# Low parts of the gates' and low-rank factors padded to 128 rows in a two-layer trunk kernel

## The chip, the cores and the metric

The kernel runs on one core of one Trainium2 chip. The metric is the device time of one execution in microseconds (us). TensorE is called PE, its weight loads PEld, VectorE DVE, ScalarE ACT, GpSimd POOL, and SyncE, which issues most transfers, SP.

## The reference

Two layers act on a sequence of 1024 frames with 1024 channels, in float32, each inside `x + norm(mixer(norm(x)))`. Layer 0 runs two mixers on parts of one projection: RG-LRU and HGRN2. Layer 1 is RWKV-7. Cut to what the change touches:

```python
# layer 0, RG-LRU: a causal convolution over 4 frames, then gates in 16 blocks of 64 channels
xblk = xc.reshape(bsz, seq, 16, 64)
gate_r = sigmoid(einsum("bsni,nij->bsnj", xblk, w_a) + b_a)
gate_i = sigmoid(einsum("bsni,nij->bsnj", xblk, w_x) + b_x)
log_a = -8 * gate_r * softplus(-lam)
h = linear_scan(exp(log_a), sqrt(-expm1(2 * log_a)) * (gate_i * xc))
...
# layer 1, RWKV-7: decay and learning rate from factors of rank 64
w_log = -softplus(-(w0 + tanh(mixes[4] @ w1) @ w2)) - 0.5
decay = exp(-exp(w_log))
iclr = sigmoid(a0 + (mixes[5] @ a1) @ a2)
```

The gates' matrices are 64x64, and `w2` and `a2` have 64 rows. Both are the short products of this case. The rest of layer 1 is a delta-rule state per head, worked out in chunks of 64 frames.

## The kernel before

Every float32 product is made of several passes on PE. A number is split into a high part that PE takes exactly (`hi`, rounded by a copy on ACT) and the rest (`lo`, a subtraction); a product then is high by high, high by low and low by high. A dense product of 128 output channels by 512 frames (`dense_t2`, L160 to L162) is 8 x 3 such passes, each 128 rows by 128 columns of weights against 512 columns. Weights come from memory in units; `load_unit` (L131 to L135) loads two tiles of 128x1024, makes the high part on ACT and the low part on POOL.

**Short factors.** With only 64 rows, the first two passes go into one: the rows 64 to 127 of the array take the same weights once more, and the moving tile holds the high part in one half and the low part in the other. So high by high and high by low are one pass of 128 rows (L644 for the gates, L1160 and L1163 for the low-rank factors). Low weights by high data is a pass of 64 rows, which uses one half of the array's rows (L645, L1161, L1164); which half depends on the block, `r = 64h to 64h+63`.

**The gates, `rglru` (L586 on).** The 8 tiles of 128 channels (`e`) are worked in four groups (`j`) of two. For each `e` and each half `th` of the frames: the dense product into PSUM, a copy to `XP` on ACT (L629), the convolution on DVE (L632, L635) into `xc`, the split of `xc` into `xs` (L641, L642), the two gate passes for each `h` on PE, and tanh on ACT (L647), then L648. There are four `xc` buffers, so all are taken in one group. After that come the second dense product of the group (the SiLU gate, L655 and L656), and for the four instances a chain on ACT and DVE (L661 to L665) into the tile `T`, one square root for all four (L667), the multiplications by `T` (L670), the scans (L671), a product (L674), and the transfer of the result to memory (`mgd`). `T` and `a2` are the last tiles of the pool `rg`.

**After it, `out0`.** The output projection of layer 0 multiplies the 16 tiles of `mgd`, in the order k = 8 to 15, then 0 to 7. For the first half of the frames each is loaded (L696, at raised priority) into a buffer of the pool `ut` (8 buffers, at the other end of the memory), split on ACT (L149) and DVE (L150), and used in passes L720 to L722. The first pass of each PSUM bank belongs to k = 8.

**The low-rank factors, `prep` (L1151 on).** Layer 1 makes 16 preparations, one for each `e` and `th`, spread over the dense products for k: a preparation begins with its four short passes into two PSUM tiles (L1160, L1161 for the decay, L1163, L1164 for the learning rate). A tanh (L1167) writes `SG`; DVE adds 1 and scans it into `GC` (L1173, L1174); ACT writes two exponentials of `GC`, `E1` (L1179) and `E2` (L1181), the second into SG's own buffer. `E2` is read by `BT` on DVE (L1195) and `KTt` on POOL (L1201). 32 passes of 64x64 (L1208) multiply BT into PSUM; ACT copies them to `AB` (L1212), and SP writes AB out in two transfers (`abf`, L1219). `SG` and `AB` have two buffers each. Passes of a 128x64 tile (L1228) add sums over heads. The first pieces of the following product use the tag `AB` for their output.

**What sets the order.** The program is written in the order of its loops, with generators that interleave parts by hand. A planner then places each instruction in the queue of its engine by a simulated run of the program, and inserts the waits; each queue is served in its order on the chip. Tiles live in pools; a pool's memory is reused by later pools, and a tile whose bytes belonged to an earlier tile waits for that tile's last reader. Pools on the left are stacked upwards, those marked right downwards.

Of the kernel before, what the change touches and what calls it, by code (L numbers as in the profile page):

```python
# [7 lines left out]
F32 = mybir.dt.float32  # L8
F32R = mybir.dt.float32r
# [7 lines left out]
P = 128  # L17
S = 1024
D = 1024
KT = D // P  # L20
# [25 lines left out]
class Net:  # L46
# [539 lines left out]
    def rglru(self, cx, uh, ul):  # L586
        tc, nc, a = self.tc, self.nc, self.a

        c = sp = cx.enter_context(self.pool("rgc", 1))
        lam = self.vec[:, VIDX["lam"]:VIDX["lam"] + KT]  # L590
# [21 lines left out]
        for bn in ("ba", "bx"):  # L612
            t = c.tile([P, KT], F32, name="h" + bn)
            for h in range(2):
                r = slice(64 * h, 64 * h + 64)
# [4 lines left out]
        for j in range(4):  # L620
            wx = self.unit() if j else None
            inst = []
            for e2 in range(2):
                e = 2 * j + e2
                XP = rp.tile([P, 4 + S], F32, name="XP", bufs=2)
                nc.gpsimd.memset(XP[:, 0:4], 0.0)
                for th in range(2):
# [11 lines left out]
                    for h in range(2):  # L639
                        r, r2 = slice(64 * h, 64 * h + 64), slice(64 - 64 * h, 128 - 64 * h)  # L640
                        nc.vector.tensor_copy(xs[r, h], xc[r])  # L641
                        nc.vector.tensor_sub(xs[r2, h], xc[r], xs[r, h].bitcast(F32))  # L642
                        ps = self.pss.tile([P, HALF], F32, name="sm")
                        nc.tensor.matmul(ps, lhsT=self.gh[:, e, h], rhs=xs[:, h], start=True, stop=False)  # L644
                        nc.tensor.matmul(ps, lhsT=self.gl[r, e], rhs=xs[r, h], start=False, stop=True)  # L645
                        for i, q in ((0, r), (1, r2)):
                            nc.scalar.activation(g[i][r], ps[q], AF.Tanh, scale=0.5, bias=hb[i][q, e:e + 1])  # L647
# [3 lines left out]
            for e2 in range(2):  # L651
                for th in range(2):
                    ps = self.dense_t(wg, e2, uh, ul, th)
# [238 lines left out]
    def layer1_proj(self):  # L892
# [12 lines left out]
        with ExitStack() as cx:  # L905
            mp = self.mx
            with ExitStack() as c2:
                lp = c2.enter_context(self.pool("lora", 1))

                self.l2h = [lp.tile([P, D], F32R, name=f"l2h{i}") for i in range(2)]  # L910
                self.l2l = lp.tile([P, D], F32R, name="l2l")
                self.LT = [lp.tile([P, S], F32R, name=f"LT{i}") for i in range(2)]
                with ExitStack() as c3:
# [4 lines left out]
                    for i in range(2):  # L918
                        r, r2 = slice(64 * i, 64 * i + 64), slice(64 - 64 * i, 128 - 64 * i)
                        nc.gpsimd.tensor_copy(self.l2h[i][r], l2[r])  # L920
                        nc.gpsimd.tensor_copy(self.l2h[i][r2], l2[r])
                        nc.gpsimd.tensor_sub(self.l2l[r], l2[r], self.l2h[i][r].bitcast(F32))
                    self.lora_parts(0, self.LT0)
# [19 lines left out]
                with ExitStack() as c3:  # L943
# [18 lines left out]
                    order = [(j, th) for j in range(2) for th in range(2)] + [(2, 0), (3, 0), (2, 1), (3, 1)]  # L962
                    w, self.mt, self.vgb, self.vgt = {}, kp, 2, "AB"
                    self.mixt = "KK"
# [15 lines left out]
                    for i in range(6):  # L980
                        run = advance()
                        self.vgt = ("AB", "R", "KP")[i // 2]
                        next(vg)
                        next(v1, None)
                        if i < 4:
                            next(v1, None)
# [164 lines left out]
    def prep(self, kp, e, th, pk):  # L1151
# [8 lines left out]
        nc.tensor.matmul(pw, lhsT=self.l2h[0][:, es], rhs=LT[0][:, sl], start=True, stop=False)  # L1160
        nc.tensor.matmul(pw, lhsT=self.l2l[0:64, es], rhs=LT[0][0:64, sl], start=False, stop=True)  # L1161
        pa = self.pss.tile([P, HALF], F32, name="l")
        nc.tensor.matmul(pa, lhsT=self.l2h[1][:, es], rhs=LT[1][:, sl], start=True, stop=False)  # L1163
        nc.tensor.matmul(pa, lhsT=self.l2l[64:128, es], rhs=LT[1][64:128, sl], start=False, stop=True)  # L1164

# [43 lines left out]
        if (e, th) == (KT - 1, 1):  # L1209
            self.norms(kp)  # L1210
        AB = kp.tile([P, 8, 64], F32, name="AB")
        nc.scalar.copy(AB, ps)  # L1212
# [410 lines left out]
```

## Time and profile before

| | us |
|---|---|
| median of 3 runs | 1886.89 |
| lowest and highest of them | 1884.31, 1889.57 |
| the profiled execution: its own time | 1885.01 |
| the profiled execution: first to last instruction (span) | 1882.9 |

| busy in the profiled execution | us | share of the span |
|---|---|---|
| PE | 1737.0 | 92% |
| PE weight loads | 1462.9 | 78% |
| DVE | 1212.2 | 64% |
| ACT | 795.6 | 42% |
| POOL | 695.8 | 37% |

The mean granted clock of TensorE is 0.95 of full speed.

How to read the lines: a row of the timeline has the start in us, the duration in us, the engine, the line of the kernel, the operation, output and inputs by the program's names, the part of the array in rows*columns (PE only), the shapes, and how many instructions are merged; in brackets the idle time of the engine ahead of it and what ended it. The ends of PE's products are modelled and overlap the following ones, so two starts tell more than a duration. "SPq" is the issue of a transfer. A row of the table of stretches has, for each engine, the busy time and the count of instructions in it. A row for one line gives the count, the shortest, median and longest duration in ns, and the first and last start.

### The profile page before, as it was taken

How to read it: one execution, taken by the hardware profiler on the slowest of the kernel's cores; microseconds unless marked ns; L12 is line 12 of the kernel's file. 1: busy time of each engine (PE TensorE's matmuls, PEld its weight loads, DVE VectorE, ACT ScalarE, POOL GpSimd, SP SyncE). 2: the span in 40 equal slices, each digit the busy share in tenths (PEclk: the TensorE clock that was granted, in tenths of full speed). 3: DMA queues.
4: the chain of work that ended last, by engine and by line, in shares of the span. 5: the costliest groups of instructions: out<-in, count | busy, mean ns of one | idle time of the engine just before them, and what ended most of it. 6: DMA issues, size and time to landing. Idle time of an engine off the chain costs nothing. (4 is left out here: it accounts for less than half of the span.)

```text
span 1882.9 us, 36336 instructions
## 1 busy us (share of the span) xinstructions
PE 1737.0 (92%) x14418; PEld 1462.9 (78%) x14418; DVE 1212.2 (64%) x2213; ACT 795.6 (42%) x1550; POOL 695.8 (37%) x618
## 2 busy tenths in 40 slices
PE   8989989999899999999999999978679999997888
PEld 6879789787897777777878766668678998875776
DVE  6485483675847889745354686786593434359985
ACT  5322222323226655445454765764453433432221
POOL 5534232333222212465434244554441425425430
PEclk9999999999899999999999999979878998988989
DMA  5101101111022111365235276654565655544531
GB/s 181 45 23 46 56 19 63 46 35 41 18 73 85 53 60 67 125 238 169 101 123 185 89 171 167 173 130 113 121 164 139 170 148 165 156 132 150 181 106 62
DMA packets 218313, 206.56 MB, mean 110 GB/s; under 512 B 133280, under 2 KB 162208, under 8 KB 218144
## 3 DMA queue, kind: packets, MB, share of 16 engines
q1 hardware_dynamic: 216992, 200.04, 35.5%
q0 software_dynamic: 1152, 4.19, 0.7%
q8 instruction: 114, 1.87, 0.4%
q14 instruction: 55, 0.45, 0.1%
HBM read 136.22 MB, written 67.96 MB: 108 GB/s over the span
## 5 line engine op out<-in xcount | busy, mean ns | idle before, releaser
L135 POOL TENSOR_TENSOR wl<-w,wh 128x1024 fp32r<-128x1024 f32 x110 | 276.5, 2520 | 291.6 <-ACT wh L133 283.2
L160 PE MATMUL mm<-xh,wh 128*128 128x512 f32 x768 | 306.3, 400 | 0.2
L162 PE MATMUL mm<-xh,wl 128*128 128x512 f32 x768 | 305.3, 398 | 0.0
L161 PE MATMUL mm<-xl,wh 128*128 128x512 f32 x768 | 304.1, 396 | 0.0
L184 PE MATMUL mm<-wh,xh 128*128 128x256 f32 x560 | 169.8, 304 | 7.5 <-ACT xh L149 3.7
L160 PEld LDWEIGHTS mm<-xh,wh 128*128 128x128 f32 x768 | 146.0, 190 | 35.3 <-issue 3.6
L162 PEld LDWEIGHTS mm<-xh,wl 128*128 128x128 f32 x768 | 145.9, 190 | 34.5 <-issue 4.1
L161 PEld LDWEIGHTS mm<-xl,wh 128*128 128x128 f32 x768 | 145.9, 190 | 33.2 <-issue 3.4
L186 PE MATMUL mm<-wh,xl 128*128 128x256 f32 x560 | 166.4, 300 | 4.9 <-DVE xl L150 4.9
L133 ACT CAST wh<-w 128x1024 fp32r<-128x1024 f32 x112 | 117.7, 1051 | 124.2 <-PE mm L161 54.8
L185 PE MATMUL mm<-wl,xh 128*128 128x256 f32 x560 | 165.7, 296 | 0.0
L184 PEld LDWEIGHTS mm<-wh,xh 128*128 128x128 f32 x560 | 114.5, 205 | 10.7 <-ACT xh L149 4.3
L186 PEld LDWEIGHTS mm<-wh,xl 128*128 128x128 f32 x560 | 113.6, 204 | 7.0 <-DVE xl L150 6.3
L185 PEld LDWEIGHTS mm<-wl,xh 128*128 128x128 f32 x560 | 114.2, 204 | 0.9
L803 DVE SCALAR_TENSOR_TENSOR mix<-ut,vec,mix 128x512 f32<-128x512 f32 x64 | 62.5, 985 | 39.9 <-ACT mix L802 39.1
L1438 POOL TENSOR_TENSOR BS<-BK,egc 128x1024 f32<-128x1024 f32 x16 | 31.7, 1980 | 139.5 <-PE pt L1443 70.7
L184 PE MATMUL po<-wh,xh 128*128 128x256 f32 x256 | 75.7, 296 | 1.6 <-DVE vg L1021 1.6
L420 DVE COPY_PREDICATED ST<-m_l,sm 64x128 f32<-64x128 uint8 x224 | 72.5, 337 | 5.5
L185 PE MATMUL po<-wl,xh 128*128 128x256 f32 x256 | 75.2, 294 | 0.0
L186 PE MATMUL po<-wh,xl 128*128 128x256 f32 x256 | 74.8, 292 | 0.0
L1428 PE MATMUL pg<-GM,BK 64*128 64x128 f32 x512 | 58.0, 308 | 9.4 <-DMA BK<-bkd 4.8
L1295 DVE TENSOR_TENSOR PR<-YP,BL 128x64 f32<-128x64 f32 (+14 forms) x60 | 57.5, 973 | 11.2 <-POOL BL L1285 10.4
(378 smaller groups left out, 4332.6 us busy)
## 6 DMA issues: line engine op xcount, KB each, us to landing
w<-in_W SPq DMA_DIRECT2D x112, 512.0 KB, 3.8
ard<-AR SPq DMA_DIRECT2D x16, 512.0 KB, 4.1
BK<-bkd SPq DMA_DIRECT2D x16, 512.0 KB, 3.7
vd<-vg SPq DMA_DIRECT2D x32, 256.0 KB, 2.7
GM<-ard SPq DMA_DIRECT2D x32, 256.0 KB, 4.4
x<-in_x SPq DMA_DIRECT2D x8, 512.0 KB, 9.8
mgd<-sgq SPq DMA_DIRECT2D x16, 256.0 KB, 2.1
ut<-mgd SPq DMA_DIRECT2D x16, 256.0 KB, 4.1
```

The lines of the kernel that those rows point to most:

```text
L133: nc.scalar.copy(hi, w)
L135: (nc.vector if first else nc.gpsimd).tensor_sub(lo, w, hi.bitcast(F32))
L160: nc.tensor.matmul(ps, lhsT=wh[:, c:c + P], rhs=a, start=(k == 0), stop=False)
L161: nc.tensor.matmul(ps, lhsT=wh[:, c:c + P], rhs=b, start=False, stop=False)
L162: nc.tensor.matmul(ps, lhsT=wl[:, c:c + P], rhs=a, start=False, stop=(k == KT - 1))
L184: nc.tensor.matmul(ps, lhsT=a, rhs=h, start=(k == 0), stop=False)
L185: nc.tensor.matmul(ps, lhsT=a, rhs=l, start=False, stop=False)
L186: nc.tensor.matmul(ps, lhsT=b, rhs=h, start=False, stop=(k == KT - 1))
L420: nc.vector.copy_predicated(d, m, x)
L803: nc.vector.scalar_tensor_tensor(out, sh, self.v(f"mu{p}", k), out, ALU.mult, ALU.add)
L1295: nc.vector.tensor_mul(fv(PR, 0, [[16 * n, 2], [n, 16], [1, n]]), fv(YP, 0, [[256, 2], [16, 16], [1, n]]), fv(BL, i, [[256, 2], [0, 16], [ ...
L1428: nc.tensor.matmul(ps[h][:, q, :], lhsT=BK[hs, eg * 4 + q, :], rhs=GM[hs, h, eg * 4 + q, :], start=True, stop=True)
```

## The change

The gates' low factor `gl` stays as it was, and `rglru` makes from it, at its start and on POOL, a tile `gl2` of 128 rows for each `e` and `h`: one half of the rows holds the low part, the other half is zero. The pass L645 then takes all 128 rows of `xs`, high and low part. The rows that held nothing are multiplied by zero.

The low-rank factors get two tiles `l2l` in place of one, each with the half that isn't used set to zero on POOL, and the passes L1161 and L1164 take all 128 rows. The second `l2l` needs 4 KB per partition. `AB` no longer has a tile: the copy L1212 writes into SG's buffer, and the pieces that used the tag `AB` use `SG`.

```diff
     def rglru(self, cx, uh, ul):
+        gl = cx.enter_context(self.pool("rgl", 1)).tile([P, KT, 2, P], F32R, name="gl2")
+        for h in range(2):
+            r, r2 = slice(64 * h, 64 * h + 64), slice(64 - 64 * h, 128 - 64 * h)
+            nc.gpsimd.memset(gl[r2, :, h].bitcast(F32), 0.0)
+            nc.gpsimd.tensor_copy(gl[r, :, h], self.gl[r].bitcast(F32))
...
-                        nc.tensor.matmul(ps, lhsT=self.gl[r, e], rhs=xs[r, h], start=False, stop=True)
+                        nc.tensor.matmul(ps, lhsT=gl[:, e, h], rhs=xs[:, h], start=False, stop=True)
...
-                self.l2l = lp.tile([P, D], F32R, name="l2l")
+                self.l2l = [lp.tile([P, D], F32R, name=f"l2l{i}") for i in range(2)]
...
-                        nc.gpsimd.tensor_sub(self.l2l[r], l2[r], self.l2h[i][r].bitcast(F32))
+                        nc.gpsimd.memset(self.l2l[i][r2].bitcast(F32), 0.0)
+                        nc.gpsimd.tensor_sub(self.l2l[i][r], l2[r], self.l2h[i][r].bitcast(F32))
...
-                    w, self.mt, self.vgb, self.vgt = {}, kp, 2, "AB"
+                    w, self.mt, self.vgb, self.vgt = {}, kp, 2, "SG"
...
-                        self.vgt = ("AB", "R", "KP")[i // 2]
+                        self.vgt = ("SG", "R", "KP")[i // 2]
...
-        nc.tensor.matmul(pw, lhsT=self.l2l[0:64, es], rhs=LT[0][0:64, sl], start=False, stop=True)
+        nc.tensor.matmul(pw, lhsT=self.l2l[0][:, es], rhs=LT[0][:, sl], start=False, stop=True)
...
-        nc.tensor.matmul(pa, lhsT=self.l2l[64:128, es], rhs=LT[1][64:128, sl], start=False, stop=True)
+        nc.tensor.matmul(pa, lhsT=self.l2l[1][:, es], rhs=LT[1][:, sl], start=False, stop=True)
...
-        AB = kp.tile([P, 8, 64], F32, name="AB")
+        AB = c3(SG)
         nc.scalar.copy(AB, ps)
```

## The prediction

> **What bounds the kernel now.** First the page's shares, then the table of stretches (PE, PEld, DVE, ACT, POOL busy with counts, then granted clock, DMA share, GB/s), cut where the two groups of changed products run: 577 to 753 us (the gates, L645) and 1064 to 1222 us (the low-rank factors, L1161 and L1164).
>
> ```profile
> PE 1737.0 (92%) x14418; PEld 1462.9 (78%) x14418; DVE 1212.2 (64%) x2213; ACT 795.6 (42%) x1550; POOL 695.8 (37%) x618
> ```
> ```profile
> 545.00:577.00 32.00, 32.00 (x166) 27.23 (x165) 17.72 (x28) 9.08 (x13) 12.74 (x11) 1.00 0.39 132
> 577.00:600.00 23.00, 23.00 (x88) 15.70 (x87) 16.51 (x27) 21.70 (x32) 0.41 (x2) 1.00 0.07 24
> 577.00:753.00 176.00, 168.94 (x671) 125.41 (x669) 147.34 (x193) 114.49 (x154) 32.34 (x17) 0.98 0.17 57
> 764.00:1064.00 300.00, 291.95 (x1309) 238.91 (x1308) 147.89 (x159) 143.17 (x237) 133.45 (x100) 1.00 0.44 150
> 1064.00:1222.00 158.00, 151.35 (x919) 106.31 (x917) 122.31 (x137) 102.06 (x166) 71.61 (x73) 0.98 0.64 160
> 1222.00:1260.00 38.00, 25.93 (x189) 20.72 (x187) 34.59 (x35) 23.47 (x42) 25.49 (x20) 0.64 0.61 159
> ```
>
> PE is busy 96% of both stretches, so it looks like the bound; but DVE is busy 84% and 77% there, and the question is how soon it becomes the bound when PE gets shorter. From 764 to 1064 us PE has 8 us of gaps: what delays PE there delays the end.
>
> Then the products themselves, and the order of time around one.
>
> ```profile
> L645 PE MATMUL sm<-xs,gl x32: 491/493/532, 577.3 to 752.9; 64*128 64x512 f32 x32
> L1161 PE MATMUL l<-LT,l2l x16: 491/498/502, 1065.4 to 1219.8; 64*128 64x512 f32 x16
> L1164 PE MATMUL l<-LT,l2l x16: 491/498/501, 1066.3 to 1222.3; 64*128 64x512 f32 x16
> ```
> ```profile
> 576.79 0.39 PE L161 MATMUL mm<-xl,wh 128*128 128x512 f32 x1
> 576.79 0.19 PEld L644 LDWEIGHTS sm<-xs,gh 128*128 128x128 f32 x1
> 577.02 0.40 PE L644 MATMUL sm<-xs,gh 128*128 128x512 f32 x1
> 577.34 0.18 PEld L645 LDWEIGHTS sm<-xs,gl 64*128 64x128 f32 x1 [0.36 <-issue]
> 577.34 0.49 PE L645 MATMUL sm<-xs,gl 64*128 64x512 f32 x1
> 577.76 0.19 PEld L162 LDWEIGHTS mm<-xh,wl 128*128 128x128 f32 x1 [0.24 <-issue]
> 577.77 0.50 PE L162 MATMUL mm<-xh,wl 128*128 128x512 f32 x1
> 578.11 0.39 PE L644 MATMUL sm<-xs,gh 128*128 128x512 f32 x1
> ```
>
> Durations overlap, so starts are read. Between two full products 0.23 us pass (576.79 to 577.02), and the weights are in before the second starts. With the 64-row product they are 0.32 (577.02 to 577.34), 0.43 (to 577.77) and 0.34 (to 578.11): its weights, and those of the next, are loaded only as it starts. One low product costs 0.09 + 0.20 + 0.11 = 0.40 us above an ordinary one.
>
> **The change part by part.** *Padding.* 64 products lose 0.40 us: 25.6 us of PE time, 12.8 in each stretch. The padded product still streams 512 columns, so it costs the ordinary 0.23. Beside 64x64 products (L1208) a change of tile stays; I take 12.4 for the second stretch.
>
> The Trainium skill, "TensorEngine Tiling (Array Packing)", section "Key Properties", says that every change of tiling mode drains the array, which would hold for the 128x64 tile of L1228 too. Where such a product follows a low one, the exit would stay priced: at most 32 x 0.2 = 6 us less. This case's rows, 0.23 us on both sides, do not show that drain:
>
> ```profile
> 1096.63 0.39 PE L160 MATMUL mm<-xh,wh 128*128 128x512 f32 x1
> 1096.86 0.40 PE L1228 MATMUL n<-sl,sel 128*64 128x512 f32 x1
> 1097.09 0.39 PE L161 MATMUL mm<-xl,wh 128*128 128x512 f32 x1
> ```
>
> *What of the first 12.8 us is on the path.* A group j of the gates has eight pairs of products, each needing xs from DVE (L642). For group 2 and the last pair of group 3:
>
> ```profile
> 672.30 0.47 PE L644 MATMUL sm<-xs,gh 128*128 128x512 f32 x1 [2.59 <-DVE xs L642]
> 693.80 1.40 DVE L642 TENSOR_TENSOR xs<-xc,xs 64x512 fp32r<-64x512 f32 x2
> 697.99 0.39 PE L644 MATMUL sm<-xs,gh 128*128 128x512 f32 x1
> 726.92 0.47 PE L644 MATMUL sm<-xs,gh 128*128 128x512 f32 x1 [2.51 <-DVE xs L642]
> 748.47 1.40 DVE L642 TENSOR_TENSOR xs<-xc,xs 64x512 fp32r<-64x512 f32 x2
> 752.57 0.39 PE L644 MATMUL sm<-xs,gh 128*128 128x512 f32 x1
> ```
>
> At a group's first pair PE waits for DVE (2.59, 2.51 us); at its last, PE is late: xs is ready at 695.20 and 749.87, the product runs 2.79 and 2.70 us later. DVE meanwhile goes on with the next step of its own chain, and the next group's xc buffers come free only after this group's scan. So per group only the lateness at the last pair can be had, some 2.6 us in groups 2 and 3; the rest turns into longer waits at the next first pair. In group 0 ACT is full (21.70 of 23 us), so I estimate 0.3; in group 1, half-way, 0.5. Sum 6 us, between 2 (ACT takes that too) and 12.8.
>
> *Building the padded gate factor.* Two fills and two copies on POOL of 64x1024:
>
> ```profile
> L582 POOL CAST gh<-gates x4: 604/607/622, 35.9 to 53.5; 64x512 fp32r<-64x512 f32 x4
> ```
>
> A copy is twice 0.607, so all four at most 4.9 us. POOL has 19 idle us from 545 to 577, before the first L645; behind them in POOL's queue stand L135's low weight halves and XP's fill. Taken as nothing; without that cover up to 4.9 us. The two fills of l2l stand on POOL with the other preparations of the low-rank factor, ahead of the stage, and are half as much at most: nothing.
>
> *The 8 KB that it occupies.* A `gl2` is 8 x 2 x 128 x 4 = 8,192 bytes per partition, and lies below the gates' other tiles. In the allocation before, the gates' last tiles, T (8,192) and a2 (2,048), end at byte 193,600 of a partition, and the lowest of out0's `ut` buffers starts at 196,320. Moved up by 8,192, T and a2 end at 201,792 and cover that buffer. The pool hands out its buffers in order, the lowest first, to k=8, which out0's first product reads; the other seven loads are planned behind it on SP, and behind those the loads of later weights. Now all eight leave at 562 us; then they can leave only after the last read of T (L670, group 3).
>
> ```profile
> 561.99 4.03 SPq L696 DMA_DIRECT2D ut<-mgd  x8
> 763.87 0.39 PE L720 MATMUL mm<-wh,xh 128*128 128x512 f32 x1
> 774.33 2.48 DVE L670 TENSOR_TENSOR xc<-xc,T 128x512 f32<-128x512 f32 x4
> 707.68 6.92 DVE L670 TENSOR_TENSOR xc<-xc,T 128x512 f32<-128x512 f32 x4 [2.54 <-ACT T L667]
> DMA to landing us min/median/max: 2.5/4.6/6.9
> 755.15 1.14 ACT L149 CAST xh<-ut 128x512 fp32r<-128x512 f32 x2
> ```
>
> Today out0's splits (L149, L150) run ahead of that chain and L670 comes at 774.33 to 776.81. Without them it can go as in group 2: 697.99 to 707.68 is 9.7 us, then 2.5 to 6.9 for L670. That is 764.8 to 769.2, less the 6 gained: 758.8 to 763.2. A landing of 4.6 and a split of 0.57 put out0's start at 764.0 to 768.4, where PE without the wait would start at 757.9: 6 to 10.5 us idle. The clock falls after such waits (0.64 in the row from 1222 us); I estimate 2 us for that, and 2 us back from gaps behind it. Term: +8, bounds 0 (another buffer given) and +20 (776.81 as now, less 6, plus 5.2, is 776.0: 18 late, and 2 of clock).
>
> *AB in SG's buffer.* SG has two buffers; AB's copy needs KTt (L1201) and BT (L1195) to have read E2, which come before it now, but the tanh of prep n+2 (L1167) waits until prep n is done with one, today until BT (L1195).
>
> ```profile
> 1171.04 0.68 DVE L1195 TENSOR_TENSOR IC<-IC,SG 128x512 f32<-128x512 f32 x1
> 1171.82 0.69 ACT L1167 ACTIVATE SG<-l,hw 128x512 f32<-128x512 f32 x1 [0.45 <-DVE IC L1195]
> 1175.87 0.61 ACT L1181 ACTIVATE SG<-GC 128x512 f32<-128x512 f32 x1
> 1179.15 1.25 SPq L1219 DMA_DIRECT2D abf<-AB  x2
> DMA to landing us min/median/max: 2.6/2.7/4.8
> L1160 PE MATMUL l<-LT,l2h x16: 387/494/503, 1065.1 to 1219.4; 128*128 128x512 f32 x16
> ```
>
> Afterwards it waits for AB's second transfer too: issue near 1179.8, landing 2.7 later, 1182.5 instead of 1171.7. Queued behind that tanh on ACT are the splits and KK, for which PE and DVE wait. The lap is then 1182.5 - 1171.7 = 10.8 us from BT to landing, 4.7 from tanh to the end of E2, and two or three DVE steps of 0.68: 17 to 18 us, for two preps. A prep takes (1219.4 - 1065.1) / 15 = 10.3 us of PE, two take 20.6, after the change 19.0. It fits, by 1 to 2 us, on queues that each serve in order. Of 12.4 us I keep 9; bounds -12.4 and +10 (below).
>
> Sum against the profiled execution, 1885.01 us (span 1882.9): -6 + 8 - 9 = -7, 1878.0. The median of the runs lies 1.9 higher: 1880. About 0.3%, 5.7 us, is what a measurement here can tell from no change.
>
> **The rivals.** *Nothing held back.* k=8 gets a free buffer and PE sets both stages: -12.8 - 12.4, with 2 lost again, -23: 1864. For it PE's 96%; against it DVE's waits above.
>
> *DVE and ACT take it all.* The gates give 2, out0 loses 7, prep gives 4: +1, 1888.
>
> *The lap becomes the pace (slower).* If the order on ACT, DVE and SP stretches the lap beyond 19.0 us it decides, seven laps long. At 22 us the stage is 7 x (22 - 20.6) = 10 longer than now: -6 + 8 + 10 = +12, 1899. For it: BT's and AB's places between other work; against it, the estimate of 17 to 18.
>
> *T stays late.* If the rglru chain isn't hurried, out0's term is +20: -6 + 20 - 9 = +5, 1892. For it: today's order, in which L670 comes 22 us after the last pair; against it, that nothing of out0 competes with it any more.
>
> *The padding changes no pitch.* By the Trainium skill, "TensorE: Matmul & The Clock Gate", Part 3, "The mechanism", weights load beside a running product only when the row groups differ; then full products would queue as switched ones do, and little is gained. As a mechanism here: a load of 0.19 us ahead of each product leaves 0.40 where it was, 1887. The rows at 576.79 show a full load beside a full product.
>
> **How the numbers follow.** Forecast 0.43 (its own range 1872 to 1888), nothing held back 0.13, DVE and ACT 0.20, lap 0.14, T late 0.08, no pitch 0.02. Faster by over 0.3% (below 1881.2): 0.26 of the forecast, 0.13, and 0.03 of the third: 0.42. Within: 0.17 + 0.14 + 0.02 = 0.33. Slower: 0.03 + 0.14 + 0.08 = 0.25. The range 1865 to 1896 leaves out half of the first rival and most of the lap's case.
>
> **What would show it.** Right: no 64*128 product with 512 columns, pitches of 0.23 around L645's and L1161's successors; waits for xs at the groups' first pairs grown to 3 us or more; `ut` loads of k=8 to 15 behind the last L670, and a wait of 6 us or more ahead of the first L720; L1167 released by an abf transfer. Wrong: loads still near 562 us (first term too small), a prep pitch above 10.3 us (the lap), or pitches that stay at 0.3 to 0.4.

## The result, and the profile after

The changed kernel takes 1919.24 us, the median of four runs (1908.12 to 1922.07); the kernel before, beside it, takes 1888.23 us (1884.31 to 1892.55). The ratio is 1.0153, with a 95% interval of 1.0106 to 1.0200: slower by 31 us, where 1880 was forecast. The profiled execution took 1922.07 us, its span is 1920.2. Line numbers behind the added lines are higher now: by 6 in `rglru` and up to L910, by 7 from L923 on. L645 is L651, L670 is L676, L696 is L702, L1167 is L1174, L1219 is L1226.

The products do what the change says. First the page's shares, then the table of stretches (columns as in the prediction), for the gates and for the preparations in their new place:

```profile
PE 1721.7 (90%) x14418; PEld 1463.2 (76%) x14418; DVE 1212.2 (63%) x2213; ACT 793.7 (41%) x1548; POOL 701.0 (37%) x624
```
```profile
577.00:753.00 176.00, 162.14 (x676) 130.53 (x677) 146.72 (x193) 113.69 (x156) 32.23 (x17) 0.95 0.16 57
1081.00:1249.00 168.00, 149.62 (x921) 110.25 (x920) 124.60 (x137) 102.37 (x167) 75.48 (x75) 0.94 0.65 156
```

PE is busy 15.3 us less in all and 6.8 less in the gates' stretch, and the span is 37.3 longer. So what was taken from PE's work came back as waiting, and more. The timeline of PE around a padded pair shows the pitches, and the last row, from the timeline of PEld, the load of the padded weights:

```profile
749.78 0.39 PE L161 MATMUL mm<-xl,wh 128*128 128x512 f32 x1
750.01 0.40 PE L650 MATMUL sm<-xs,gh 128*128 128x512 f32 x1
750.24 0.40 PE L651 MATMUL sm<-xs,gl 128*128 128x512 f32 x1
750.48 0.39 PE L162 MATMUL mm<-xh,wl 128*128 128x512 f32 x1
...
750.01 0.19 PEld L651 LDWEIGHTS sm<-xs,gl 128*128 128x128 f32 x1
```

All starts of products are 0.23 to 0.24 us apart, where the unpadded ones were 0.32, 0.43 and 0.34, and the load runs beside the product ahead of it. The next two rows, from the groups by line, are the first product of a gates' pair, after and before: behind the first bar stand busy time and mean ns, behind the second the idle time ahead of it.

```profile
L650 PE MATMUL sm<-xs,gh 128*128 128x512 f32 x32 | 15.3, 477 | 14.0 <-DVE xs L648 14.0
```
```profile
L644 PE MATMUL sm<-xs,gh 128*128 128x512 f32 x32 | 13.1, 408 | 7.1 <-DVE xs L642 7.1
```

PE's wait for xs doubled, from 7.1 to 14.0 us. Of the 12.8 us that the products lost, DVE took back 6.9 at once. From the first gates' product to the last it takes 173.5 us in place of 175.5.

Then comes the largest single hole. The timeline of the engines between the gates and out0 (ACT, DVE, SP's issues, PE):

```profile
758.05 1.92 ACT L673 ACTIVATE T<-T 128x2048 f32<-128x2048 f32 x1
760.00 6.80 DVE L676 TENSOR_TENSOR xc<-xc,T 128x512 f32<-128x512 f32 x4 [2.26 <-ACT T L673]
...
773.11 1.48 DVE L680 TENSOR_TENSOR sgr<-xc,sgr 128x512 f32<-128x512 f32 x2
...
769.66 2.10 SPq L681 DMA_DIRECT2D mgd<-sgr  x2
771.87 0.37 SPq L131 DMA_DIRECT2D w<-in_W  x1
774.01 0.92 SPq L681 DMA_DIRECT2D mgd<-sgr  x2
774.98 6.29 SPq L702 DMA_DIRECT2D ut<-mgd  x9
...
779.58 0.62 ACT L149 CAST xh<-ut 128x512 fp32r<-128x512 f32 x1 [15.23 <-DMA ut<-mgd]
...
780.25 0.80 PE L726 MATMUL mm<-wh,xh 128*128 128x512 f32 x1 [18.71 <-ACT xh L149]
```

The chain that uses T is hurried, as forecast: its last multiplication ends at 766.80 us, 10 us earlier than before. But the loads don't leave then. On SP they stand behind the four stores of the group's results (L681), and these wait for the scans and products that follow (to 774.59). They leave at 774.98, the first lands 4.6 us later, and PE has stood still for 18.71 us. Before, they left at 562 us.

In the preparations the profile shows what the lap's rival described. The tanh of the preparations by line, after (L1174) and before (L1167), and one lap, from the tanh of one preparation to that of the next but one:

```profile
L1174 ACT ACTIVATE SG<-l,hw 128x512 f32<-128x512 f32 x16 | 11.0, 686 | 17.4 <-DMA abf<-SG 17.4
```
```profile
L1167 ACT ACTIVATE SG<-l,hw 128x512 f32<-128x512 f32 x16 | 11.0, 689 | 10.6 <-DVE IC L1195 10.6
```
```profile
1180.24 0.69 ACT L1174 ACTIVATE SG<-l,hw 128x512 f32<-128x512 f32 x1 [1.67 <-DMA abf<-SG]
...
1183.22 0.61 ACT L1188 ACTIVATE SG<-GC 128x512 f32<-128x512 f32 x1
...
1186.36 0.68 ACT L1197 ACTIVATE KK<-mm,vec 128x512 f32<-128x512 f32 x1
...
1188.71 0.69 DVE L1202 TENSOR_TENSOR IC<-IC,SG 128x512 f32<-128x512 f32 x1
...
1197.84 0.58 ACT L1219 COPY SG<-s 128x512 f32<-128x512 f32 x1
1198.45 1.25 SPq L1226 DMA_DIRECT2D abf<-SG  x2
1202.00 0.69 ACT L1174 ACTIVATE SG<-l,hw 128x512 f32<-128x512 f32 x1 [1.77 <-DMA abf<-SG]
```

From tanh to tanh it is 21.76 us for two preparations, and what ends the waits is the landing of AB's transfer, where it was BT on DVE before. The pitch over all sixteen is 11.00 us in place of 10.28.

The rest lies where the change has no line. The span falls into four stages, each measured from its own start, so that a late start of one doesn't count twice (the stretch ahead of the gates' first product is alike within 0.2 us):

| us, profiled executions | before | after | difference |
|---|---|---|---|
| A: first gates' product to out0's first | 186.9 | 203.1 | +16.2 |
| B: out0's first product to the first preparation's | 301.2 | 301.1 | -0.1 |
| C: first preparation's product to the last AB copy | 191.7 | 195.3 | +3.6 |
| D: last AB copy to the end | 626.2 | 643.6 | +17.4 |

D is as large as A. There, the groups by line show for the g pieces' product (po) and for the norms of the finished chunks (m):

```profile
L184 PE MATMUL po<-wh,xh 128*128 128x256 f32 x256 | 77.0, 301 | 18.7 <-DVE vg L1028 18.7
L1519 DVE TENSOR_REDUCE m<-yn 128x8 f32<-128x512 f32 x15 | 10.3, 683 | 30.0 <-DMA yn<-yd 30.0
```

and for the kernel before:

```profile
L184 PE MATMUL po<-wh,xh 128*128 128x256 f32 x256 | 75.7, 296 | 1.6 <-DVE vg L1021 1.6
L1512 DVE TENSOR_REDUCE m<-yn 128x8 f32<-128x512 f32 x15 | 10.2, 680 | 17.8 <-DMA yn<-yd 17.7
```

PE waits 18.7 us in place of 1.6 for a DVE multiplication, and DVE waits 30.0 in place of 17.7 for a load. One place of the timeline (SP, DVE, PE) shows how the two belong together:

```profile
1443.68 8.00 SPq L1311 DMA_DIRECT2D wd<-YP  x14
...
1456.03 0.43 SPq L1507 DMA_DIRECT2D yn<-yd  x1
...
1462.25 0.69 DVE L1519 TENSOR_REDUCE m<-yn 128x8 f32<-128x512 f32 x1 [14.19 <-DMA yn<-yd]
...
1464.60 0.41 DVE L1028 TENSOR_TENSOR vg<-po,vg 128x256 f32<-128x256 f32 x1
...
1465.07 0.58 PE L184 MATMUL po<-wh,xh 128*128 128x256 f32 x1 [10.05 <-DVE vg L1028]
```

DVE stands for 14.19 us in the norm of chunk 0, whose load is late because SP issues 14 small stores and five other loads first. In DVE's queue the multiplication L1028, which would free PE's bank, stands behind the norm's first two instructions.

The same waits show in the stretch D as a whole, before and after (columns as in the table of stretches):

```profile
1256.75:1882.90 626.15, 551.58 (x7151) 487.73 (x7151) 383.88 (x658) 233.44 (x589) 224.22 (x183) 0.91 0.49 137
```
```profile
1276.64:1920.20 643.56, 545.99 (x7146) 480.31 (x7145) 388.06 (x660) 236.03 (x591) 229.01 (x185) 0.91 0.48 135
```

PE is not busier in the longer stretch, and the granted clock is 0.91 in both. So D grew by idle time of PE, 97.6 us in place of 74.6, and not by a lower clock.

### The profile page after: what moved, and what is told of

Same layout as the page of the kernel before. It is cut to its first block, busy times and chain, and to the rows that moved or that the text cites. A ratio compares the mean times of both kernels' runs of the same rounds, so it can differ in the third digit from the quotient of the medians.

```text
span 1920.2 us, 36383 instructions
## 1 busy us (share of the span) xinstructions
PE 1721.7 (90%) x14418; PEld 1463.2 (76%) x14418; DVE 1212.2 (63%) x2213; ACT 793.7 (41%) x1548; POOL 701.0 (37%) x624
## 5 line engine op out<-in xcount | busy, mean ns | idle before, releaser
L135 POOL TENSOR_TENSOR wl<-w,wh 128x1024 fp32r<-128x1024 f32 x110 | 273.5, 2492 | 299.7 <-ACT wh L133 280.5
L184 PE MATMUL po<-wh,xh 128*128 128x256 f32 x256 | 77.0, 301 | 18.7 <-DVE vg L1028 18.7
L726 PE MATMUL mm<-wh,xh 128*128 128x512 f32 x128 | 52.2, 408 | 18.7 <-ACT xh L149 18.7
L184 PEld LDWEIGHTS po<-wh,xh 128*128 128x128 f32 x256 | 50.9, 199 | 20.8 <-DVE vg L1028 19.1
L1515 POOL TENSOR_TENSOR V<-V,ln 128x512 f32<-128x512 f32 x16 | 20.7, 1295 | 117.1 <-DMA V<-vd 54.5
```

Source lines behind the costliest of these rows:

```text
L135: (nc.vector if first else nc.gpsimd).tensor_sub(lo, w, hi.bitcast(F32))
L184: nc.tensor.matmul(ps, lhsT=a, rhs=h, start=(k == 0), stop=False)
L726: nc.tensor.matmul(ps[t4], lhsT=mh[k][:, sl], rhs=h, start=first, stop=False)
```

## The experiments

The theory after the result: the loss is two places in memory (gl2 pushing T over a ut buffer, AB in SG's buffer), and a last phase whose queues are planned in another order. The rivals: the padded products themselves cost; the last phase is longer because out0 is late; one half of the change does it all. The table has all runs; A to D are the stages above, B included in "A+B"; they come from the one profiled execution of each kernel, which lies 9 us below the median for "low-rank, AB in E1" and 9 and 10 us above it for "before, norms held" and "gates' half, norms held", and within 6 us of it elsewhere. The ratio is to the kernel before on the same chip, with its 95% interval. "Ahead" is the number of g pieces' multiplications (L1028) that DVE does before the norms of chunk 0 and chunk 1, counted in the trace.

| kernel | median us | ratio (interval) | A | A+B | C | D | ahead |
|---|---|---|---|---|---|---|---|
| before | 1888.23 | | 186.9 | 488.1 | 191.7 | 626.2 | 8, 11 |
| the change | 1919.24 | 1.0153 (1.0106 to 1.0200) | 203.1 | 504.1 | 195.3 | 643.6 | 4, 10 |
| gates' half | 1917.56 | 1.0159 (1.0143 to 1.0174) | 203.0 | 503.9 | 191.6 | 644.1 | 9, 13 |
| its memory alone | 1923.90 | 1.0197 (1.0178 to 1.0215) | 207.0 | 507.6 | 193.1 | 645.3 | 9, 13 |
| low-rank half | 1893.30 | 1.0031 (1.0008 to 1.0054) | 188.1 | 490.6 | 197.0 | 626.6 | 8, 11 |
| AB in SG alone | 1894.16 | 1.0036 (1.0015 to 1.0058) | 186.8 | 489.3 | 197.3 | 633.5 | 8, 11 |
| low-rank, AB in E1 | 1911.71 | 1.0142 (1.0119 to 1.0165) | 186.8 | 488.9 | 189.2 | 645.7 | 9, 13 |
| T in XP, gates padded | 1885.57 | 0.9993 (0.9982 to 1.0004) | 180.3 | 487.6 | 190.0 | 630.4 | 8, 11 |
| T in XP alone | 1875.40 | 0.9943 (0.9928 to 0.9958) | 181.3 | 481.1 | 192.1 | 622.3 | 8, 11 |
| both paddings, both places mended | 1910.14 | 1.0120 (1.0101 to 1.0140) | 180.4 | 484.7 | 190.5 | 652.6 | 9, 13 |
| the change, T in XP | 1892.90 | 1.0039 (1.0022 to 1.0056) | 180.3 | 484.8 | 198.3 | 631.5 | 8, 11 |
| the change, norms held | 1921.83 | 1.0185 (1.0170 to 1.0201) | 202.4 | 503.6 | 194.6 | 646.2 | 29, 29 |
| both mended, norms held | 1890.24 | 1.0026 (1.0011 to 1.0042) | 180.4 | 487.4 | 191.5 | 633.0 | 31, 31 |
| before, norms held | 1895.36 | 1.0044 (1.0025 to 1.0062) | 189.1 | 491.9 | 190.4 | 643.3 | 29, 29 |
| gates' half, norms held | 1909.43 | 1.0144 (1.0105 to 1.0183) | 203.5 | 506.6 | 195.5 | 641.8 | 31, 31 |
| T in XP, two taps out | 1882.11 | 0.9985 (0.9969 to 1.0002) | 180.6 | 490.2 | 192.4 | 630.3 | 8, 11 |
| the same, gates padded | 1874.85 | 0.9945 (0.9926 to 0.9963) | 171.7 | 479.1 | 190.7 | 632.6 | 8, 11 |
| T in XP, split on POOL | 1879.70 | 0.9964 (0.9946 to 0.9982) | 181.8 | 483.9 | 190.9 | 623.0 | 8, 11 |
| the same, gates padded | 1884.02 | 0.9993 (0.9976 to 1.0010) | 180.5 | 486.0 | 190.2 | 626.8 | 8, 11 |

**The halves and their side effects.** Four kernels take the change apart.

The gates' half:

```diff
+        gl = cx.enter_context(self.pool("rgl", 1)).tile([P, KT, 2, P], F32R, name="gl2")
...
+                        nc.tensor.matmul(ps, lhsT=gl[:, e, h], rhs=xs[:, h], start=False, stop=True)
```

> Only the gates' half of the change: the padded gl2 (8 KB per partition) and full products for the gates; low-rank factors and AB as before. Theory 'held loads': out0's eight ut loads stand behind the stores of the last gates' group on SP, the first product of out0 starts at 778 to 782 us in place of 763.9, and the end comes 15 to 18 us later than before, about 1903, with the stage of the low-rank factors at its old pitch of 10.3 us a preparation. Rival 'everything after 1276 us grows because of what this half does': the end is 30 us later or more, 1918. Rival 'the loss lies in the low-rank half': 1880 to 1886, as the gates' products gain 2 us.

Measured: out0 starts at 780.02 us, and A, B and C are as the theory said, but the end is 30 us later, which was the first rival's figure. D is 644.1 us in this kernel too, with no edit in the low-rank factors.

The low-rank half (padded l2l, AB in SG's buffer):

```diff
+                self.l2l = [lp.tile([P, D], F32R, name=f"l2l{i}") for i in range(2)]
...
+        AB = c3(SG)
```

> Only the low-rank half: padded l2l, AB in SG's buffer, pieces on the tag SG; gates as before. Theory 'lap': the two-preparation lap is 21.9 us or more, the pitch 10.9 to 11.2 us a preparation against 10.3, L1174 of the changed kernel released by abf; the AB copy of the last preparation is 3 to 5 us later than before. If the further 17 us of the changed kernel after 1276 us come from this half, the end is 18 to 22 us later, about 1907; if they come from the gates' half or from chance, 1890 to 1893. Rival 'no lap': pitch 9.5 to 9.8 us, 1878.

Measured: the pitch is 11.03 us, C is 5.4 us longer, D is unchanged (626.6): 1893.30, at the edge of the second case. D's growth isn't of this half.

AB's place without padding:

```diff
-        AB = kp.tile([P, 8, 64], F32, name="AB")
+        AB = c3(SG)
```

> Only the copy AB in SG's buffer and the pieces on the tag SG; all products as before. Theory 'lap': the tanh of a preparation still waits for the abf transfer of the one before the last, and the pitch is 10.9 to 11.4 us, the same as with padding, so the end is no better than that of the low-rank half alone: 1890 to 1893 if the later drift isn't of it, 1905 to 1910 if it is. Rival 'the loss is in the padded products or the fills': pitch 10.3, 1886 to 1889.

Measured: pitch 11.02 us, C 197.3, 1894.16. With or without padding the lap is the same, so it is AB's place that sets it. The group of the tanh in this kernel says so in one row:

```profile
L1167 ACT ACTIVATE SG<-l,hw 128x512 f32<-128x512 f32 x16 | 11.0, 686 | 15.5 <-DMA abf<-SG 15.5
```

The memory of gl2 without gl2:

```diff
+        pad = cx.enter_context(self.pool("rgl", 1)).tile([P, KT, 2, P], F32, name="pad")
+        nc.gpsimd.memset(pad[:, 0, 0, 0:4], 0.0)
```

> Before, with a tile of 8 KB per partition that nothing reads where gl2 would lie; all products as before. Theory 'held loads': the ut loads are held as with gl2, out0 starts 14 to 18 us later than before, near 780, and the end is 15 to 18 us later, about 1904. Rival 'it is the changed order of products, not the memory': out0 starts near 764, and the time is that of before, 1886 to 1889.

Measured: out0 starts at 781.96 us with the products unpadded, 1923.90 in all, above both cases. 8 KB that nothing reads cost about as much as the whole change (36 us against 31, with intervals that overlap). The gates' half is 6.3 us faster than this kernel, 4.0 of them in A: that is what the padding gives beside the held loads.

**The two places mended.** T in the XP buffers, with the gates padded:

```diff
+            TT = [rp.tile([P, 4 + S], F32, name="T", tag="XP", bufs=2)[:, 0:S].rearrange("p (i t) -> p i t", i=2) for _ in range(2)]
...
+            for T in TT:
+                nc.scalar.activation(T, T, AF.Sqrt, scale=1.0 / 16)
```

> The gates' half with its memory given back: gl2 as in the change, but T lies in the two XP buffers (two tiles of two instances each, two square roots in place of one), so the gates' tiles end where they did and cover no ut buffer; low-rank factors as before. Theory 'held loads': the ut loads leave near 562 us again, out0's first product comes at 756 to 764 us, and the 16 us are gone. Two theories of the further growth after 1276 us: if a late out0 makes it, it is gone as well and the end is 1878 to 1884; if any change of the queues' order in front makes it, 8 to 20 us of it stay and the end is 1886 to 1900. Rival 'the padded products themselves cost': 1895 or more, with out0 still 10 us late or more.

Measured: out0's first product at 758.05 us, D 630.4, 1885.57. The 16 us are gone, and most of D's growth with them.

Its control, without padding:

> The control of the run with T in the XP buffers: that edit alone, all products and AB as before. It changes the order of the queues but not the time at which out0 can start. If only a late out0 makes the last phase longer: out0 starts at 762 to 766 us, the time from the last AB copy to the end is that of before (626 us) within 3, the total 1884 to 1890, and the padded one is 4 to 8 us faster. If order alone does: 632 us or more from the last AB copy to the end and 1892 or more.

Measured: 1875.40, faster than both kernels of this study. The order in front changed, and D stayed short (622.3), so not any change of order lengthens it. But neither theory had the main thing: the padded one is 10 us slower. Both start out0 after the same 180 to 181 us; the padded one reaches the first preparation 6.5 us later (3.71 of them are one wait in out0's first passes, for DVE's SiLU gate L662) and has 8 us more in D. What makes these 8 is not shown.

AB in E1's buffer:

```diff
-        AB = kp.tile([P, 8, 64], F32, name="AB")
+        AB = E1[:, :, 1:65]
```

> The low-rank half with another place for AB: padded l2l, but AB is copied into E1's buffer (columns 1 to 64 of each 65), which is written 4 to 5 us later in a preparation than SG; pieces on the tag SG; gates as before. Theory 'lap': from E1's exponential to the landing is 17 to 18 us for two preparations in place of 21.9, so no wait for abf stands in the pace, the tanh is released by PE or DVE again, and the pitch falls to 9.4 to 9.9 us; the last AB copy is 5 to 10 us earlier than before and the end 1877 to 1884. Rival 'DVE and ACT set the pace': pitch 10.1 to 10.4, the last AB copy within 3 us of before, 1884 to 1890. Rival 'the lap stays': pitch above 10.6, 1892.

Measured: the tanh waits for BT again, as before the change, but the wait for AB's transfer is not gone. It has moved to E1's exponential (E in the trace), which stands ahead of KK in ACT's queue:

```profile
L1168 ACT ACTIVATE SG<-l,hw 128x512 f32<-128x512 f32 x16 | 11.0, 688 | 15.6 <-DVE IC L1196 15.4
L1180 ACT ACTIVATE E<-GC 128x512 f32<-128x512 f32 x16 | 10.1, 631 | 13.7 <-DMA abf<-E 9.6 <-DVE GC L1175 4.0
```

The pitch is 10.18 us and C 2.5 us shorter than before: the figures of the rival "DVE and ACT set the pace". But its cause isn't shown, since a shorter lap through AB's transfer is still there; of 12.4 us of shorter products 2.5 arrive. The end was missed by all three cases: D is 645.7 us, with out0 at 763.70 us.

Both together:

> Both paddings, with T in the XP buffers and AB in E1's. If the loss of the change is the two places in memory alone and the last phase grows only with a late out0, the gains of both halves add: 5 from the gates and 5 to 8 from the preparations, 1873 to 1879, faster than before. If the preparations are bound by DVE and ACT: 1880 to 1884. If any new order of the last phase costs: 1886 to 1896.

Measured: A to C are 4.5 us shorter in sum than before, out0 starts at 755.38 us, and D is 652.6: 1910.14, above every case. So a late out0 isn't needed for a long D; the theory that tied it to the lateness fell here.

**The last phase.** The column "ahead" separates the kernels without an edit in the last phase: with 8 and 11, D is 622 to 634 us (nine edited kernels and the one before), with 9 and 13 or 4 and 10 it is 644 to 653 (five). Four kernels with an edit there ask whether the place of these norms is the cause. The edit gives the norms of chunks 0 and 1 a late input:

```diff
             y = gp.tile([P, HALF], F32, name="yn")
+            if ch < 2:
+                nc.vector.tensor_copy(y[:, 0:1], self.last[:, 0:1])
```

> The changed kernel with one edit in the last phase: the norms of chunks 0 and 1 (L1519 on) get one element of chunk 7's output copied into their tile before its load, so they can't be placed in DVE's queue ahead of the early g pieces' multiplications (L1028). Theory 'order of the queues': in the changed kernel DVE stands in these norms and waits for their load, while PE waits for L1028 (gaps of 10.1 and 8.7 us, at 1455 and 1599 us); without that the time from the last AB copy to the end falls from 643.6 us to 625 to 632, and the whole to about 1903 to 1908. Rival 'a late out0 or a lower clock makes the last phase longer': it stays at 640 us or more, and the whole at 1915 or more.

Measured: the rival's figures, D 646.2 us and 1921.83. In the trace, PE's wait for L1028 is gone (0.5 us), and the results of chunks 6 to 8 are stored 5.6 to 7.4 us earlier than in the changed kernel; then PE idles 12.88 us from 1676 us on for a merge. ACT's queue stands there for a load of output weights, ahead of the merge's copy:

```profile
1686.84 1.14 ACT L149 CAST xh<-w 128x512 fp32r<-128x512 f32 x2 [13.64 <-DMA w<-in_W]
1687.88 1.08 ACT L1347 COPY W<-pi 16x128 f32<-16x128 f32 x4
```

> Both paddings with T in the XP buffers and AB in E1's, as in the run with both places mended, plus the held norms. Theory 'order of the queues': the 652.6 us from the last AB copy to the end fall to 625 to 635, the whole from 1910 to 1886 to 1892. Rival: no change in it, 1905 or more.

Measured: as the theory said, D falls from 652.6 to 633.0 us and the whole from 1910.14 to 1890.24. PE's waits at the g pieces, without and with held norms:

```profile
L184 PE MATMUL po<-wh,xh 128*128 128x256 f32 x256 | 77.0, 301 | 14.5 <-DVE vg L1029 14.5
```
```profile
L184 PE MATMUL po<-wh,xh 128*128 128x256 f32 x256 | 75.0, 293 | 0.0
```

> The control: the kernel before with the held norms alone. Theory 'order of the queues': PE doesn't wait for the norms there, so little is to be had: from the last AB copy to the end 622 to 628 us against 626.2, the whole 1883 to 1889. Rival 'holding the norms is a gain in any order': 10 us or more faster, 1877 or less.

Measured: outside both cases, 1895.36, slower than before by 0.44%. Its profiled execution is 9 us slower than its median and shows D of 643.3 us. Holding the norms is no gain by itself: it gives this kernel another order too.

The change with one place mended, T in the XP buffers:

> The whole change, AB in SG's buffer included, with one edit: T in the XP buffers, so that no ut buffer is covered. Theory: what is lost at out0 (16 us) is gone, the lap stays (6 us, as in the low-rank half alone), and in DVE's queue the two early norms stand behind 8 and 11 g pieces, as before, so the last phase has its old length, 622 to 634 us: 1888 to 1894 in all. Rival 'the last phase grows with the padding or with a changed memory': 640 us or more, and 1903 or more.

Measured: 1892.90, in the theory's range. This is the whole change without the covered buffer, and its loads leave as early as before:

```profile
560.13 4.00 SPq L703 DMA_DIRECT2D ut<-mgd  x8
```

Of the change's 31 us some 24 go with this edit, for it is 7 us slower than the kernel before on the same chip; what stays is C, 198.3 us, the lap.

The gates' half with held norms was to part the late out0 from the order:

> The gates' half alone, where out0 is 16 us late and the last phase took 644.1 us, with the norms of chunks 0 and 1 held until chunk 7. In DVE's queue they stand behind 31 g pieces, as in the mended kernel with held norms, whose last phase took 633.0 us. Theory 'order of the queues': 625 to 635 us from the last AB copy to the end, though out0 is as late as before (778 to 782 us), and the whole 1905 to 1910. Rival 'a late out0 makes it': 642 to 648 us, and 1915 to 1920.

Measured: unclear. The median, 1909.43, is in the theory's range and 8 us below the gates' half (6 when each is compared with the kernel before on its chip); the profiled execution, the slowest of its four (1919.62), shows D of 641.8 us, next to the rival's. Whether a late out0 adds something of its own is left open.

The traces allow one more comparison, of the order in which DVE, ACT, POOL and SP do their work in D. Instruction for instruction it is the same in the kernel before and in the six with T in the XP buffers and AB in its own tile, padded or not, taps out or not; D is 622.3 to 632.6 us there. A second order stands in the three with AB in SG's buffer and no covered `ut` buffer (626.6 to 633.5), a third in the gates' half and its memory alone (644.1 and 645.3), a fourth in the two with AB in E1's buffer (645.7 and 652.6). The change has an order of its own, and so has each kernel with held norms. So the order follows the places of the tiles and not the padding, and kernels with one order lie within some 10 us of each other. With held norms the column "ahead" is nearly alike (29 or 31) and D is not (633.0 to 646.2): the place of these two norms is not the whole of it.

**Where the gates' 12.8 us went.** Two kernels that leave two of the convolution's taps out:

```diff
-                    for q in (2, 1, 0):
+                    for q in (0,):
```

> A kernel that leaves work out: of the convolution's four taps two are left out (L635 runs once in place of three times), which takes 32 x 0.82 = 26 us from DVE in the gates' stage; T in the XP buffers, no padding. It is the base for the next one. Theory 'DVE sets the gates' pace': from the first gates' product (577 us) to out0's first product it takes 3 to 9 us less than the 181.4 us of the kernel with T in the XP buffers, and PE waits less than 2 us for xs in 577 to 747 us. Rival 'PE sets it already': the same 181 us within 2.

> The same with the two taps left out, and with the gates' padding. Theory 'DVE's pace took the gates' gain': with DVE relieved, PE sets the pace and the padding shortens the time from the first gates' product to out0's first product by 8 to 12.8 us against the kernel with the taps left out alone. Rival 'the padded products gain nothing on PE, or ACT sets the pace': 0 to 4 us.

Measured: less DVE work alone brings nothing to A (180.6 us against 181.3), so there the rival holds; with the padding it brings 8.9 us, and 11.1 by the first preparation. The 11.1 hold against this base alone, whose B is the longest of all (309.6 us, against 299.8 with T in XP and all taps); against T in XP alone the padded one is 2.0 us ahead there. The stretch from 577 to 753 us in four kernels, T in XP alone, then padded:

```profile
577.00:753.00 176.00, 172.29 (x695) 128.65 (x694) 157.48 (x201) 129.66 (x173) 33.16 (x18) 0.99 0.18 63
```
```profile
577.00:753.00 176.00, 163.32 (x693) 130.63 (x692) 156.14 (x200) 126.32 (x169) 33.43 (x18) 0.98 0.17 58
```

and the same two with the taps left out:

```profile
577.00:753.00 176.00, 175.30 (x722) 133.72 (x722) 134.22 (x173) 132.16 (x177) 37.62 (x21) 1.00 0.20 67
```
```profile
577.00:753.00 176.00, 173.80 (x756) 142.67 (x755) 142.73 (x187) 137.68 (x188) 40.06 (x22) 0.99 0.23 74
```

With all taps, padding leaves PE as many products in the stretch (695 and 693) and 9 us of idling. With the taps out it gets 34 products further (722 to 756) and stays busy. PE and DVE are both near their limit here: shortening DVE's work alone moves A by 0.7 us, shortening PE's alone by 1.0, shortening both by 9.6.

The last pair tried that in a whole kernel, with the second block's subtraction on POOL:

```diff
-                        nc.vector.tensor_sub(xs[r2, h], xc[r], xs[r, h].bitcast(F32))
+                        (nc.gpsimd if h else nc.vector).tensor_sub(xs[r2, h], xc[r], xs[r, h].bitcast(F32))
```

> Unpadded, T in the XP buffers, and of the two subtractions that split xs (L642) the one of the second block goes to POOL: 16 x 0.95 = 15 us less on DVE, the whole is computed. The base for the padded one. By the kernel with taps left out, PE and DVE are both near their limit in the gates' stage, and a shorter DVE alone brings at most 1 to 2 us: first gates' product to out0's first product 179 to 182 us, the whole 1874 to 1880. Rival 'POOL is late with its half and PE waits for it': 184 us or more.

> The same with the gates' padding. Theory 'the gain needs both, shorter products and a relieved DVE': 5 to 11 us less from the first gates' product to out0's first product than without padding, and the whole 5 to 11 us faster than it: 1866 to 1872, below both kernels of the study and below the 1875.4 us of T in the XP buffers alone. Rival 'ACT or POOL takes the place of DVE': within 3 us of the unpadded one.

Measured: A is 181.8 and 180.5 us, as the rival said; the padded kernel is slower by 4.3 us, outside both cases. DVE's busy time in the stretch is 159.4 us with 20 instructions fewer than the 157.5 of T in XP alone, because its other instructions got longer (last section). The move didn't relieve DVE, so the pair doesn't test the theory; it shows that this way isn't one.

## Why the prediction was wrong, step by step

**Pitch of the padded products: right.** 0.23 us, with a full load beside a full product. The rival "the padding changes no pitch" is out.

**The gates' -6: right in kind, too large.** The prediction said that per group "only the lateness at the last pair can be had" and summed 6. In the changed kernel the last product of the stretch came 2.0 us sooner. DVE is nearer its limit than the step allowed for: with T out of the way, padding gives 1.0 us in A, and it takes a lighter DVE to make it 8.9. That the rest turns into waits for xs was forecast, and they grew to 14.0 us.

**out0's +8: the failed step.** All eight loads held and the hurried chain came as described. That a covered buffer holds them is borne out by the 8 KB tile and by T in the XP buffers; the byte addresses stand in no trace. The step that failed is "A landing of 4.6 and a split of 0.57 put out0's start at 764.0 to 768.4". It lets the loads go when T has been read. That had an end at 766.80, 3.6 us after the forecast's latest; but the loads stood on SP behind stores that wait for work after T, and left 8.2 us later still. A is 16.2 us longer though the gates took 2.0 less, so the term is +18.2 against +8. The bound of +20 was there, under the wrong mechanism (T late in DVE's queue, which didn't happen). The kernel with 8 KB that nothing reads, and those with T in XP, show that this term belongs to the memory and not to the padded products.

**The preparations' -9: the failed step was the lap.** "17 to 18 us, for two preps" took BT for a few DVE steps after E2. BT also needs KK, the dense product that ACT copies at 1186.36, 2.5 us after E2's end (1183.83), and then DVE's place for it: from E2's end to BT's start it is 4.9 us, against two or three steps of 0.68. From BT's end (1189.40) to the next tanh it is 12.6 us, against the 10.8 of the forecast. AB's copy alone is 8.4 us away, since its 64x64 products wait on PE and the copy behind KK of the next preparation on ACT. The lap is 21.76 us. The rival's 22 was an example and not worked out, so this hit is luck. Its price was too high at the end of the stage: the sixteenth preparation starts 10.7 us later in its row (15 pitches of 11.00 against 10.28, about the 10 that the rival had), but its AB copy only 3.6: before, that copy came 37.4 us behind the preparation's first product, now 30.4. What the shorter products would bring without any lap no run shows: with AB in E1's buffer they bring 2.5 us of C and not 12.4, but there E1's exponential waits for AB's transfer.

**The last phase: not in the sum at all.** The prediction has no term behind the preparations, so it took everything there as moving rigidly, without a reason; this stretch holds 17.4 of the 37.3 us. The runs show that D differs by up to 30 us among kernels (622.3 to 652.6) with the same work in it; that it does so with out0 on time; that 8 KB alone do it; that kernels with one order of the queues lie within some 10 us; and that in one kernel holding two norms, which reorders the queues, takes 20 us away. So the cause is the order into which the planner puts the queues, which reacts to edits far ahead. Not shown are why it takes the one order or the other, which part of an order costs the time in each kernel, and whether a late out0 adds something by itself.

Added up, the steps missed by 4 us in the gates, 10 at out0, 13 in the preparations and 17 behind them. That is the 44 us between the forecast's -7 and the 37 that lie between the two profiled executions; between the forecast and the median it is 39, since the forecast put the median 1.9 us above the profiled execution, and the profiled execution after is slower than its median by 2.8.

## What to carry to other kernels

A tile that moves memory is an edit of every later tile that its neighbours come to cover: look up what lies above it, and price the release by the queue of the engine that issues the next load (what stands ahead of it there, and what those wait for), not by the semaphore alone. Work taken from an engine whose partner is just as full comes back as waiting, so pair it with work taken from the partner, and test that with a kernel that leaves the partner's work out. Where a planner orders the queues, compare stages from their own starts and expect stages that the edit doesn't touch to change (here one of 626 us, by 17). Read from the traces whether the queues there still have the same order; a control with the edit's side effect alone tells them from the edit. And when a wait is mended by moving a tile, look for the same wait at the tile's new place.

## What the runs showed of the hardware

After its 18.71 us of idling PE runs its first products at half speed, 0.43 us from start to start, and from 786 on at 0.23. The table of stretches has the granted clock in the column after POOL:

```profile
780.00:783.00 3.00, 2.75 (x7) 2.17 (x8) 2.39 (x2) 2.42 (x5) 3.00 (x2) 0.50 1.04 389
783.00:786.00 3.00, 3.00 (x9) 2.38 (x8) 3.00 (x5) 2.10 (x4) 0.16 (x1) 0.54 0.75 271
786.00:789.00 3.00, 3.00 (x15) 2.48 (x14) 2.53 (x6) 1.77 (x3) 0.00 (x0) 1.00 0.92 246
```

Seven starts lie 0.42 to 0.43 us apart, one 0.60 and one 0.34, in place of 0.23. That is an estimated 1.9 us lost; the prediction had put down 2.

Work moved from DVE to POOL made other instructions of DVE longer. The subtraction takes 1.73 us on POOL, and DVE's multiplication beside it (L648, two inputs) goes from 0.69 to 1.18 us in the mean; T in XP alone, then with the split on POOL, both from 577 to 753 us:

```profile
L648 DVE SCALAR_TENSOR_TENSOR xc<-gate,xc 128x512 f32<-128x512 f32 x16 | 11.0, 688 | 4.8 <-ACT gate L647 4.6
```
```profile
L642 POOL TENSOR_TENSOR xs<-xc,xs 64x512 fp32r<-64x512 f32 x15 | 26.0, 1732 | 59.5 <-DVE xs L641 54.4 <-PE sm L645 5.1
L648 DVE SCALAR_TENSOR_TENSOR xc<-gate,xc 128x512 f32<-128x512 f32 x15 | 17.7, 1183 | 3.9 <-ACT gate L647 3.7
```

The Trainium skill, "SBUF — State Buffer", section "Who interferes with whom", states that a DVE instruction with two inputs from that memory contends with a GpSimd instruction that reads it; these rows agree, at 0.49 us an instruction on the mean. One by one, the nine of the sixteen L648 that meet no POOL instruction take 0.66 to 0.69 us; the six that start while POOL subtracts take 1.06 to 1.68 us and end 0.55 us after it; one that starts during a subtraction for the weights (L135) takes 2.89.
